# A four-layer transformer kernel on one core: modulation units in three parts, written order for a tail's second stream, an earlier context norm

## Chip, cores and metric

The kernel runs on one core of one Trainium2 chip. The metric is the device time of one execution in microseconds (us). PE is TensorE's matrix engine, DVE is VectorE, ACT is ScalarE, POOL is GpSimd, and SP is the engine whose queue issues the loads.

## The reference

Two latent streams of 256 tokens of 1024 features are worked on: the latents ("LAT") and a context ("CTX"). Four layers follow one another. The first two come from `first_block`, the others from `second_block` (one mLSTM layer, one sliding-window attention layer). Each layer computes its modulation from the condition vector, mixes tokens, and runs an MLP with a fourfold hidden width:

```python
mod = silu_c @ w_mod[l] + b_mod[l]                 # 1024 -> 6 * 1024, for latents and context
a = modulate(rms_norm(h, norm1_g[l]), sh1, sc1)    # h * (1 + scale) + shift
...
h = h + g1 * mix                                   # mix: pooling, gating unit, attention, or mLSTM
h = h + g2 * sq_relu_mlp(modulate(rms_norm(h, norm2_g[l]), sh2, sc2), w_ff1[l], w_ff2[l])
```

The context goes through the same steps in layers 1 and 3; layers 2 and 4 only read it.

## The kernel before

Everything is one program of `Builder` methods. Activations lie with features on partitions, in 8 tiles of 128 features by 512 columns: 256 of the context, 256 of the latents. Every operand of a large product is split into a high part and a low part (`whi` and `wlo` for weights), and three matmuls are issued for each 128x128 block: high by high, high by low, low by high. A weight block of 128x1024 is loaded by SP's queue into `raw`, copied by ScalarE to `whi`, and subtracted by VectorE (or the engine in `wlow`) to give `wlo`. `STAGES` gives each of `raw`, `mraw`, `whi` and `wlo` three buffers.

`gemm` takes the output tiles in turn; with `head=3` the first three run interleaved in `rows_of`, two steps apart (`SKEW`), so that TensorE has work while the inputs of the next step are made. With `tail` the last tiles run one stream after the other in `last_tiles`. `Steps` lets a norm's instructions (the mean rows, then the rstd rows of `ident`) be issued in between at given steps: `PRE` in heads, `MID` in tails. `issue_after` fixes the order of instructions; without it a scheduler picks, on each engine, the next instruction by its estimate of readiness.

The modulation is 352 units of 128 input features by 512 output features. One unit loads `mraw`, multiplies it by the condition and adds it to the sum `macc` on VectorE (context), multiplies it on ScalarE and adds it to a second sum on GpSimd (latents); after eight units a few small matmuls with `sel` reduce `macc` into `acc`. `drip` issues units between weight blocks at a rate `b.rate`, and `need(i, cg)` issues all that are left of a group when its result is wanted:

```python
    def one(self):
        self.pending.pop(0)[1]()

    def need(self, i, cg):
        while any(key == (i, cg) for key, _ in self.pending):
            self.one()
```

`block1` is layers 1 and 2 (l = 0 and 1), the mLSTM layer is layer 3, and the layer whose queries come from `project(t)` is layer 4.

## Time and profile before

| | |
|---|---|
| runs | 2252.66, 2251.72, 2252.01 us, median 2252.01 |
| profiled execution | 2251.2 us |
| its span, first to last instruction | 2249.3 us |
| mean granted TensorE clock | 0.986 |
| PE busy | 2179.0 us, 97% |
| DVE, ACT, POOL busy | 1617.5, 1155.4, 642.3 us |
| moved by DMA | 337.86 MB, mean 150 GB/s |

The profiled execution is one run with the profiler on; its span leaves out 1.9 us around the instructions. TensorE's busy share is an average: in the MLPs it is full, and between them it waits. A clock of 1.00 is 2.4 GHz, of 0.50 is 1.2 GHz.

### The profile page before, as it was taken

How to read it: one execution, taken by the hardware profiler on the slowest of the kernel's cores; microseconds unless marked ns; L12 is line 12 of the kernel's file. 1: busy time of each engine (PE TensorE's matmuls, PEld its weight loads, DVE VectorE, ACT ScalarE, POOL GpSimd, SP SyncE). 2: the span in 40 equal slices, each digit the busy share in tenths (PEclk: the TensorE clock that was granted, in tenths of full speed). 3: DMA queues.
4: the chain of work that ended last, by engine and by line, in shares of the span. 5: the costliest groups of instructions: out<-in, count | busy, mean ns of one | idle time of the engine just before them, and what ended most of it. 6: DMA issues, size and time to landing. Idle time of an engine off the chain costs nothing.

```text
span 2249.3 us, 36790 instructions
## 1 busy us (share of the span) xinstructions
PE 2179.0 (97%) x13602; PEld 1861.3 (83%) x13602; DVE 1617.5 (72%) x2830; ACT 1155.4 (51%) x2176; POOL 642.3 (29%) x529
## 2 busy tenths in 40 slices
PE   9899999999999989998999999999999999999998
PEld 7777877887777778898999977778777778879998
DVE  5876656777666986789777766678775566697776
ACT  4556434544443456655555665645444433676453
POOL 1630534524221542045000234262232122421000
PEclk9999999999999999999999999999999999999999
DMA  8451535445565443367554323444455552214552
GB/s 296 140 167 36 169 122 190 144 133 183 191 193 162 147 154 127 120 215 254 166 186 151 113 85 104 142 142 131 137 187 177 173 168 80 76 48 143 186 179 93
DMA packets 129011, 337.86 MB, mean 150 GB/s; under 512 B 15040, under 2 KB 24256, under 8 KB 128832
## 3 DMA queue, kind: packets, MB, share of 16 engines
q1 hardware_dynamic: 128832, 335.51, 46.0%
q8 instruction: 108, 1.77, 0.3%
q14 instruction: 71, 0.58, 0.1%
HBM read 334.40 MB, written 1.05 MB: 149 GB/s over the span
## 4 chain that ended last, share of the span: by engine, by line
PE 46%; DVE 4%; ACT 2%; issue 2%; POOL 1%; DMA 0%; DVEq 0%; POOLq 0%; ACTq 0%
PE mm L124 28%; PE mx L124 11%; PE S L124 2%; PE T L124 1%; PE num L124 1%; PE pv L124 1%; PE T L128 1%; DVE wlo L132 1%; ACT whi L118 1%; PE acc L124 0%; POOL macc L480 0%; DMA mraw<-wmod_in 0%; PE kv L124 0%; DVE B L121 0%; ACT W L118 0%
## 5 line engine op out<-in xcount | busy, mean ns | idle before, releaser
L124 PE MATMUL mm<-A,whi 128*128 128x512 f32 (+2 forms) x2632 | 666.2, 340 | 4.9 <-DVE A L121 1.5
L480 POOL TENSOR_TENSOR macc<-macc,mraw 128x512 f32<-128x512 f32 x244 | 361.9, 1483 | 757.3 <-ACT mraw L118 744.8
L124 PEld LDWEIGHTS mm<-A,whi 128*128 128x128 f32 x2632 | 449.3, 190 | 69.0 <-issue 10.0
L124 PE MATMUL mm<-B,whi 128*128 128x512 f32 (+2 forms) x1916 | 461.4, 331 | 2.8 <-DVE h L121 1.0
L132 DVE TENSOR_TENSOR wlo<-raw,whi 128x1024 fp32r<-128x1024 f32 x255 | 350.8, 1378 | 140.7 <-ACT whi L118 139.6
L124 PE MATMUL mm<-A,wlo 128*128 128x512 f32 (+2 forms) x1316 | 444.4, 338 | 1.2 <-DVE wlo L132 1.2
L118 ACT ACTIVATE whi<-raw 128x1024 fp32r<-128x1024 f32 x267 | 281.2, 1055 | 250.5 <-PE mm L124 154.6
L124 PEld LDWEIGHTS mm<-B,whi 128*128 128x128 f32 x1916 | 322.1, 189 | 41.8 <-issue 3.0
L118 ACT ACTIVATE mraw<-mraw,silu 128x512 f32<-128x512 f32 x244 | 175.5, 723 | 303.1 <-DVE macc L121 181.3
L124 PE MATMUL mx<-A,whi 128*128 128x512 f32 (+2 forms) x1272 | 323.3, 341 | 5.5 <-ACT whi L118 4.2
L124 PE MATMUL mm<-B,wlo 128*128 128x512 f32 (+2 forms) x958 | 315.2, 330 | 1.1 <-DVE wlo L132 1.1
L121 DVE SCALAR_TENSOR_TENSOR macc<-mraw,silu,macc 128x512 f32<-128x512 f32 x244 | 250.2, 1025 | 58.8 <-DMA mraw<-wmod_in 56.3
L124 PEld LDWEIGHTS mm<-A,wlo 128*128 128x128 f32 x1316 | 249.4, 190 | 29.2 <-DVE wlo L132 2.0
L132 DVE TENSOR_TENSOR wlo<-Y,whi 128x1024 fp32r<-128x1024 f32 x160 | 207.7, 1298 | 78.7 <-ACT whi L118 78.5
L118 ACT ACTIVATE whi<-Y 128x1024 fp32r<-128x1024 f32 x160 | 168.9, 1055 | 177.8 <-PE mm L124 124.7
L124 PEld LDWEIGHTS mx<-A,whi 128*128 128x128 f32 x1272 | 218.6, 190 | 35.1 <-ACT whi L118 4.4
L124 PE MATMUL mx<-A,wlo 128*128 128x512 f32 (+2 forms) x636 | 216.3, 340 | 0.7 <-DVE wlo L132 0.7
L124 PE MATMUL mx<-B,whi 128*128 128x256 f32 (+2 forms) x852 | 203.9, 327 | 3.0 <-DVE B L121 1.3
L124 PEld LDWEIGHTS mm<-B,wlo 128*128 128x128 f32 x958 | 181.1, 189 | 19.9 <-DVE wlo L132 2.0
L121 DVE SCALAR_TENSOR_TENSOR h<-mm,mod,h 128x256 f32<-128x256 f32 x278 | 125.5, 478 | 65.0 <-PE mm L124 64.6
L124 PEld LDWEIGHTS mx<-B,whi 128*128 128x128 f32 x852 | 144.3, 191 | 19.9 <-DVE B L121 2.7
L551 POOL TENSOR_TENSOR sums<-sums,T 128x256 f32<-128x256 f32 x60 | 65.6, 1100 | 307.5 <-ACT T L118 306.3
(331 smaller groups left out, 3009.8 us busy)
## 6 DMA issues: line engine op xcount, KB each, us to landing
mraw<-wmod_in SPq DMA_DIRECT2D x352, 256.0 KB, 2.9
Y<-ff_in SPq DMA_DIRECT2D x160, 512.0 KB, 3.6
raw<-ff_in SPq DMA_DIRECT2D x96, 512.0 KB, 3.5
raw<-win_in SPq DMA_DIRECT2D x68, 512.0 KB, 3.8
raw<-mwin_in SPq DMA_DIRECT2D x17, 512.0 KB, 3.5
raw<-wo_in SPq DMA_DIRECT2D x16, 512.0 KB, 4.3
raw<-swin_in SPq DMA_DIRECT2D x10, 512.0 KB, 3.5
B<-wfirst_in SPq DMA_DIRECT2D x16, 256.0 KB, 6.7
```

The lines of the kernel that those rows point to most:

```text
L118: return self.nc.scalar.activation(out, in_, func, **kw)
L121: return self.nc.vector.scalar_tensor_tensor(out, a, scalar, b, op0, op1)
L124: return self.nc.tensor.matmul(out, lhsT=lhsT, rhs=rhs, start=start, stop=stop, **kw)
L128: return self.nc.tensor.transpose(out, in_, self.ident[:k, :k])
L132: (eng or self.nc.vector).tensor_sub(lo, src, hi.bitcast(F32))
L480: self.nc.gpsimd.tensor_add(a1, a1, raw)
L551: (adder or self.nc.gpsimd).tensor_add(sums, sums, sq)
```

## The change

Five things are edited. A modulation unit becomes a generator in three parts: its load; the sum on VectorE; the product on ScalarE with the sum on GpSimd. `one` issues the last part of the unit before, then the load of this unit and of the next where they aren't out yet, then this unit's sum on VectorE. `rows_of` keeps the written order whenever it has steps, not only after a given instruction, and `last_tiles` hands the tail's second stream the last instruction before it until the steps are through. `MID` goes from (6, 12) to (8, 14). Layer 1 drips no units until its v rows. Layer 2's context norm is issued at `NEXT` = (2, 5) inside the first three tiles instead of behind them, and the loads of the next weights with it. Layer 4's first two query weights get their low parts on VectorE.

```diff
--- before.py
+++ after.py
@@ -38,7 +38,9 @@
 FIRST = (3, 3, 3, 3, 5, 7, 7, 7, 7), (2, 2, 2, 2, 4, 6, 6, 6, 6), (1, 1, 1, 1, 3)
 
 WARM = 40
-PRE, MID = (4, 7), (6, 12)
+PRE, MID = (4, 7), (8, 14)
+
+NEXT = (2, 5)
 PLAIN = (3, 6)
 
 SOONER = 70
@@ -57,6 +59,9 @@
             ins = next(self.parts, None)
         return ins
 
+    def done(self):
+        return self.n >= self.at[-1]
+
     def finish(self):
         for _ in self.parts:
             pass
@@ -67,6 +72,7 @@
         self.tc, self.nc, self.io = tc, tc.nc, io
         self.n = 0
         self.pending, self.owed, self.rate = [], 0.0, 0.0
+        self.begun, self.loaded = None, []
         self.raws = cycle(["raw"])
         self.ready, self.late = [], []
         self.banks = cycle(["mm", "mm", "mx"])
@@ -167,7 +173,7 @@
 
         last = len(xs) - 1
         order = after and (lambda ins=after: self.tc.issue_after(ins.ins))
-        strict = bool(after)
+        strict = bool(after or steps)
         for i in range(r0, r1 + SKEW * (len(tiles) - 1)):
             for j, (ps, (d, w)) in enumerate(zip(pss, tiles)):
                 i0 = i - SKEW * j
@@ -185,18 +191,18 @@
                     part = steps.tick()
                 ins = part or ins
                 order = lambda ins=ins: self.tc.issue_after(ins.ins)
-            elif steps:
-                steps.tick()
         return ins
 
-    def group(self, tiles, ks_of, xs, cols, evac, steps=None):
-
-
+    def group(self, tiles, ks_of, xs, cols, evac, steps=None, after=None):
+
+
+        ins = None
         for a, e in cols:
             pss = [self.ps(next(self.banks))[:, :e - a] for _ in tiles]
-            self.rows_of(pss, tiles, ks_of, xs, 0, len(xs), a, e, steps)
+            ins = self.rows_of(pss, tiles, ks_of, xs, 0, len(xs), a, e, steps, after)
             self.flush()
             self.take(pss, tiles, a, e, evac)
+        return ins
 
     def take(self, pss, tiles, a, e, evac):
 
@@ -207,7 +213,7 @@
                     self.late.append(part)
 
     def gemm(self, aps, xs, c0, evac, head=0, tail=0, order=(LAT, CTX), pre=None, mid=None, flush=True,
-             ahead=(), streams=True):
+             ahead=(), streams=True, at=PRE):
 
 
 
@@ -223,7 +229,7 @@
                      for j in range(m)]
             if i + m == n:
                 self.ready = [self.wload(ap, KT) for ap in ahead]
-            steps = Steps(pre, PRE) if pre and i == 0 else None
+            steps = Steps(pre, at) if pre and i == 0 else None
             self.group(tiles, ks_of, xs, cols[:1], evac, steps)
             if steps:
                 steps.finish()
@@ -245,9 +251,13 @@
 
     def last_tiles(self, tiles, ks_of, xs, by_stream, evac, mid):
         steps = Steps(mid, MID) if mid else None
+        last = None
         for s, cols in enumerate(by_stream):
             for tile in tiles:
-                self.group([tile], ks_of, xs, [cols], evac, steps if s else None)
+                due = s and steps and not steps.done()
+                ins = self.group([tile], ks_of, xs, [cols], evac, steps if due else None,
+                                 last if due else None)
+                last = ins
         if steps:
             steps.finish()
 
@@ -462,7 +472,9 @@
         w, sc = self.io[f"wmod{i}"], self.silu[i // 2]
 
         def unit(cg, half, k):
+
             raw = self.staged(w[cg, k][:, half * 512:half * 512 + 512], 512, cycle(["mraw"]))
+            yield
             a0, a1 = self.macc[:, 0], self.macc[:, 1]
 
             alone = i % 2 == 1 and cg >= 2
@@ -472,6 +484,7 @@
                     self.nc.vector.tensor_scalar_mul(a0, raw, sc[:, k, s:s + 1])
                 else:
                     self.stt(a0, raw, sc[:, k, s:s + 1], a0, ALU.mult, ALU.add)
+            yield
             if not alone or k % 2:
                 if k < 2 - (not alone):
                     self.act(a1, raw, scale=sc[:, k, LAT:LAT + 1])
@@ -495,8 +508,7 @@
         out = []
         for cg in groups:
             for half in range(2):
-                out += [((i, cg), (lambda cg=cg, half=half, k=k: unit(cg, half, k)))
-                        for k in range(KT)]
+                out += [((i, cg), unit(cg, half, k)) for k in range(KT)]
         return out
 
     def drip(self):
@@ -508,12 +520,27 @@
         self.owed = min(self.owed, 1.0)
 
     def one(self):
-        self.pending.pop(0)[1]()
+
+
+        self.rest()
+        self.begun = self.pending.pop(0)[1]
+        for piece in [self.begun] + [u for _, u in self.pending[:1]]:
+            if piece not in self.loaded:
+                next(piece)
+                self.loaded.append(piece)
+        self.loaded.remove(self.begun)
+        next(self.begun)
+
+    def rest(self):
+        if self.begun:
+            next(self.begun, None)
+        self.begun = None
 
     def need(self, i, cg):
 
         while any(key == (i, cg) for key, _ in self.pending):
             self.one()
+        self.rest()
         while self.late:
             self.flush()
 
@@ -886,7 +913,7 @@
         b.perm1 = b.load(ph, "perm1")
         b.icnt = b.load(ph, "icnt")
     pscale = b.vec[l][:, 64:66]
-    b.rate = 0.0 if l else RATES[l][0]
+    b.rate = 0.0
     win = io[f"win{l}"]
 
     qs, kh, kl = [], [], []
@@ -948,9 +975,7 @@
     if l == 0:
         pre(evac_first)
     else:
-        b.gemm(aps[:3], xs, c0, evac_first, head=3)
-        b.ready = [b.wload(ap, KT) for ap in aps[3:]]
-        b.whole(pre)
+        b.gemm(aps[:3], xs, c0, evac_first, head=3, pre=pre, at=NEXT, ahead=aps[3:])
         b.gemm(aps[3:4], xs, c0, lambda j, *r: evac_first(j + 3, *r))
     b.gemm_rows(aps[4:], L, xs, ("T", "T", "S", "S")[c0 // P:], evac_vs, c0=c0)
     br = b.new_xs("B", 4)
@@ -1393,9 +1418,10 @@
     def project(t):
         b.gemm([win[t]], xs, L, lambda _, ps, a, e: qs.append(query(ps)))
 
-    b.wlow = nc.gpsimd
     project(0)
     for t in range(8):
+        if t == 1:
+            b.wlow = nc.gpsimd
         if t < 7:
             project(t + 1)
         a = b.new_xs("A", 1)[0]
```

How this moves instructions is shown at three places. A name such as `T<-mm` is output from input; numbers are those of tiles and differ between the two programs.

First, VectorE at the tail of layer 3's output projection, before, up to the pair sum (L558) and the norm's small `sm`:

```order
L132 TENSOR_TENSOR wlo_15568<-raw_15565,whi_15567 128x1024
L121 SCALAR_TENSOR_TENSOR macc<-mraw_16180,silu_72,macc 128x512
L121 SCALAR_TENSOR_TENSOR h<-mx_15571,mod_97,h 128x256
L121 SCALAR_TENSOR_TENSOR macc<-mraw_16185,silu_72,macc 128x512
L121 SCALAR_TENSOR_TENSOR h<-mm_15600,mod_97,h 128x256
L121 SCALAR_TENSOR_TENSOR macc<-mraw_16229,silu_72,macc 128x512
L121 SCALAR_TENSOR_TENSOR h<-mm_15628,mod_97,h 128x256
L558 TENSOR_TENSOR T_3078_15626<-T_3078_15626,T_3080_15654 128x256
L568 TENSOR_SCALAR sm_15681<-T_15676 128x2
```

and of the change (the pair sum is L585 there):

```order
L127 SCALAR_TENSOR_TENSOR macc<-mraw_15527,silu_72,macc 128x512
L127 SCALAR_TENSOR_TENSOR h<-mm_15492,mod_97,h 128x256 x2
L138 TENSOR_TENSOR wlo_15545<-raw_15542,whi_15544 128x1024
L127 SCALAR_TENSOR_TENSOR h<-mx_15548,mod_97,h 128x256
L127 SCALAR_TENSOR_TENSOR h<-mm_15577,mod_97,h 128x256
L127 SCALAR_TENSOR_TENSOR h<-mm_15605,mod_97,h 128x256
L585 TENSOR_TENSOR T_3074_15603<-T_3074_15603,T_3076_15631 128x256
L127 SCALAR_TENSOR_TENSOR h<-mx_15634,mod_97,h 128x256
L595 TENSOR_SCALAR sm_15664<-T_15659 128x2
```

Three modulation sums (`macc<-mraw`) stood among the gate sums `h` ahead of the pair sum; now the last one stands before two `h`, a low part and three more `h`.

Second, TensorE at the start of layer 2, before, where the rstd rows of the norm (`T<-ident`) are issued:

```order
L124 MATMUL mm_7644<-A_7316,wlo_7583 128x256
L124 MATMUL mm_7644<-A_7318,whi_7582 128x256
L124 MATMUL mm_7644<-A_7319,whi_7582 128x256
L124 MATMUL mm_7644<-A_7318,wlo_7583 128x256
L124 MATMUL T_7607<-ident_118,sm_7604 128x128 x2
L124 MATMUL mm_7644<-A_7320,whi_7582 128x256
L124 MATMUL mm_7644<-A_7321,whi_7582 128x256
L124 MATMUL mm_7644<-A_7320,wlo_7583 128x256
L124 MATMUL mm_7644<-A_7322,whi_7582 128x256
```

and of the change:

```order
L130 MATMUL mm_7457<-A_7267,wlo_7424 128x256
L130 MATMUL mx_7458<-A_7263,whi_7429 128x256
L130 MATMUL mx_7458<-A_7264,whi_7429 128x256
L130 MATMUL T_7496<-ident_118,sm_7472 128x128 x2
L130 MATMUL mx_7458<-A_7263,wlo_7430 128x256
L130 MATMUL mm_7459<-A_7259,whi_7435 128x256
L130 MATMUL mm_7459<-A_7260,whi_7435 128x256
L130 MATMUL mm_7459<-A_7259,wlo_7436 128x256
L130 MATMUL mm_7457<-A_7269,whi_7423 128x256
```

The rstd rows stood in the middle of the fourth tile (`mm_7644`, alone); now they stand in the middle of the first three tiles (`mx_7458`, `mm_7459` and `mm_7457` in turn). The mean rows ahead of them move likewise.

Third, ScalarE at layer 1's queries, before (`T<-mx` is the copy of a query tile that the rotation needs, `Y` what becomes of it):

```order
L118 ACTIVATE T_271_1390<-acc_1381 128x128
L118 ACTIVATE Y_1357<-T_265_1359 64x256 x2
L118 ACTIVATE mraw_1559<-mraw_1559,silu_71 128x512
L118 ACTIVATE T_277_1424<-mx_1398 128x256
L118 ACTIVATE Y_1423<-mx_1398 64x256
L118 ACTIVATE whi_2212<-raw_2210 128x1024
L118 ACTIVATE Y_1423<-mx_1398 64x256
```

and of the change, up to the first products:

```order
L124 ACTIVATE T_252_1295<-mm_1269 128x256
L124 ACTIVATE Y_1294<-mm_1269 64x256 x2
L124 ACTIVATE Y_1294<-T_253_1296 64x256 x2
L124 ACTIVATE whi_2154<-raw_2152 128x1024
L124 ACTIVATE T_263_1350<-mx_1324 128x256
L124 ACTIVATE Y_1349<-mx_1324 64x256 x2
L124 ACTIVATE Y_1349<-T_264_1351 64x256 x2
L124 ACTIVATE whi_2191<-raw_2189 128x1024
L124 ACTIVATE T_275_1410<-mm_1384 128x256
L124 ACTIVATE Y_1409<-mm_1384 64x256
L124 ACTIVATE macc<-mraw_1375,silu_71 128x512
L124 ACTIVATE mraw_1441<-mraw_1441,silu_71 128x512
```

A modulation product (`mraw<-mraw`) stood right ahead of the copy `T<-mx`; now the first three `T` copies come with no product among them, and the products follow the third.

## Rows read from the trace of the kernel before

**Rows 1.** the page: span, and busy time of the engines

```profile
span 2249.3 us, 36790 instructions
...
PE 2179.0 (97%) x13602; PEld 1861.3 (83%) x13602; DVE 1617.5 (72%) x2830; ACT 1155.4 (51%) x2176; POOL 642.3 (29%) x529
```

**Rows 2.** windows (columns in the second line; PEclk is the granted clock)

```profile
core 0: us, PE busy (x) PEld busy (x) DVE busy (x) ACT busy (x) POOL busy (x), PEclk, DMA share, GB/s
82.00:89.00 7.00, 5.51 (x36) 4.40 (x37) 6.28 (x10) 6.30 (x13) 3.24 (x4) 0.51 0.52 140
...
829.00:840.00 11.00, 5.99 (x25) 5.27 (x26) 10.94 (x18) 3.63 (x7) 3.35 (x5) 0.53 0.45 153
1512.00:1519.00 7.00, 6.88 (x32) 6.88 (x33) 2.42 (x6) 1.36 (x2) 2.17 (x2) 0.52 0.25 64
...
550.00:700.00 150.00, 150.00 (x684) 119.15 (x683) 97.80 (x141) 61.83 (x87) 40.97 (x29) 1.00 0.59 190
```

**Rows 3.** waits of TensorE: total us, times, longest us

```profile
PE T L124 <- DVE T L558: 6.4, 3, 3.7
PE T L124 <- ACT E L118: 6.0, 2, 5.7
PE T L124 <- ACT T L118: 4.8, 5, 2.1
PE mx L124 <- ACT whi L118: 4.2, 1, 4.2
...
PE S L124 <- DVE wlo L132: 2.8, 1, 2.8
...
PE T L128 <- DVE E L1170: 2.2, 2, 1.1
PE mm L124 <- ACT T L118: 2.1, 1, 2.1
```

**Rows 4.** timeline, layer 1's keys: start, us, engine, line [idle <- releaser]

```profile
80.48 0.72 DVE L121 SCALAR_TENSOR_TENSOR macc<-mraw,silu,macc 128x512 f32<-128x512 f32 x1
...
81.29 0.72 ACT L118 ACTIVATE mraw<-mraw,silu 128x512 f32<-128x512 f32 x1 [4.28 <-DVE sm L942]
...
82.86 0.57 ACT L118 ACTIVATE E<-mm 128x512 f32<-128x512 f32 x1
```

**Rows 5.** timeline, layer 1's queries, ScalarE and TensorE

```profile
140.46 0.72 ACT L118 ACTIVATE mraw<-mraw,silu 128x512 f32<-128x512 f32 x1 [3.12 <-issue]
...
148.72 1.04 ACT L118 ACTIVATE whi<-raw 128x1024 fp32r<-128x1024 f32 x1
149.79 0.38 ACT L118 ACTIVATE T<-mm 128x256 f32<-128x256 f32 x1
```

**Rows 6.** timeline, start of layer 2

```profile
824.82 0.33 SPq L143 DMA_DIRECT2D raw<-win_in  x1
...
829.06 2.05 ACT L118 ACTIVATE whi<-raw 128x1024 fp32r<-128x1024 f32 x2
...
825.50 3.11 DVE L121 SCALAR_TENSOR_TENSOR T<-h,A,T 128x256 f32<-128x256 f32 x5 [0.71 <-ACT T L118]
833.97 1.21 DVE L132 TENSOR_TENSOR wlo<-raw,whi 128x1024 fp32r<-128x1024 f32 x1
```

**Rows 7.** timeline, head of layer 1's up projection, VectorE

```profile
437.70 1.21 DVE L132 TENSOR_TENSOR wlo<-Y,whi 128x1024 fp32r<-128x1024 f32 x1
```

**Rows 8.** timeline, tail of layer 3's output projection, VectorE

```profile
1508.82 0.75 DVE L121 SCALAR_TENSOR_TENSOR macc<-mraw,silu,macc 128x512 f32<-128x512 f32 x1 [3.19 <-DMA mraw<-wmod_in]
...
1510.79 1.28 DVE L558 TENSOR_TENSOR T<-T,T 128x256 f32<-128x256 f32 x1 [0.82 <-ACT T L118]
```

**Rows 9.** timeline, start of layer 4, three engines

```profile
1919.76 2.37 POOL L132 TENSOR_TENSOR wlo<-raw,whi 128x1024 fp32r<-128x1024 f32 x1 [4.22 <-ACT whi L118]
...
1920.32 2.10 DVE L771 TENSOR_TENSOR T<-T,T 128x256 f32<-128x256 f32 x1
```

**Rows 10.** instructions on macc: ns min/median/max, first and last start

```profile
L480 POOL TENSOR_TENSOR macc<-macc,mraw x244: 1262/1308/2863, 55.2 to 1859.4; 128x512 f32<-128x512 f32 x122
```

## The prediction

> **What bounds the kernel now.** I read the page's busy times first. TensorE is busy 2179.0 of 2249.3 us [rows 1], so 70.3 us of idle time, a slow clock and the matmuls themselves are all that there is to win. Then the windows: in the long MLP stretches TensorE is busy all the time at a granted clock of 1.00, and nothing is to be had there; between them lie short stretches at 0.51 to 0.53, which is the lower of the clock's two levels, 1.2 GHz beside 2.4 [rows 2]. Such a stretch costs what its busy time loses: from 82 to 89 us (1 − 0.51) × 5.51 = 2.7 us, from 829 to 840 us 0.47 × 5.99 = 2.8, from 1512 to 1519 us 0.48 × 6.88 = 3.3. Each lies at one of TensorE's long waits, so a wait costs itself and often some 3 us behind it. The list of waits [rows 3] names who ends them, and the timelines around the longest [rows 4 to 6, 8, 9] what the releaser itself stood behind. The reader is to see one pattern in them: a modulation product or sum (`mraw`, `macc`), which nobody needs soon, stands ahead of the instruction that TensorE waits for.
>
> **The change, part by part.** No matmul, copy or load is added beyond a handful of rows; the sum is of waits that go and waits that come.
>
> (a) Layer 1's keys. TensorE waits 5.7 us for the copy E [rows 3], which runs from 82.86 to 83.43; on ScalarE it stands behind a product that waited 4.28 us and started at 81.29, when the sum at 80.48 was done, and a weight copy [rows 4]. At stake are 5.7 + 2.7 = 8.4 us. In three parts the unit's load no longer goes out in the same turn as its sum, and in layer 1 no unit is dripped before the v rows; yet seven products still stand ahead of this E in the new order. I take 40%, **−3.5**; bounds 0 (the seven are as slow as now) and −8.4.
>
> (b) Layer 1's queries. Of five waits for a T copy (4.8 us in all, [rows 3]) two of some 2 us lie here. ScalarE reached the first copy behind a product at 140.46 that had idled 3.12 us; the second came at 149.79, right behind a product and a weight copy [rows 5]. The new order has the T copies ahead of the products (the third piece of order above). I take **−4.0**, nearly both; bounds 0 and −5.
>
> (c) Start of layer 2. TensorE waits 4.2 us for a high part and 2.8 us for a low part [rows 3]; the first ends when ScalarE's two copies from 829.06 end, at 831.11, the second when VectorE's low part from 833.97 ends, at 835.18 [rows 6]. That low part stands behind the context's modulation, which began at 825.50. With the norm's rows inside the head, the modulation starts some 6 us sooner (an estimate: its T rows stand about 50 matmuls sooner, and 684 took 150.00 us [rows 2], with half as many columns in many here), and the 2.8 us go. The 4.2 us mostly stay: the weights' load is issued at 824.82, a buffer's release sets that, and the copies could hardly run before 828. I take 2.8 + 1.2 = **−4.0**; bounds +1 (TensorE only arrives sooner at the late load, and the clock falls the same) and −(4.2 + 2.8 + 2.8) = −9.8.
>
> (d) Tail of layer 3's output projection. The longest wait for VectorE's pair sum is 3.7 us [rows 3]: a modulation sum waited 3.19 us for its load and started at 1508.82, and the pair sum could start only at 1510.79 and took 1.28 [rows 8]. In the new order no modulation sum stands within five instructions ahead of it (first piece of order), and MID moves the mean rows six matmuls later, 6 × 150.00 / 684 = 1.3 us at most. With the clock 3.7 + 3.3 = 7.0 us are at stake. Written order keeps TensorE from filling at the second tail tile, whose four mean rows now stand together; for that I keep back 2.5: **−4.5**, bounds −1 and −7.
>
> (e) Start of layer 4. TensorE waits 2.1 us for a T copy [rows 3]. GpSimd's low part (1919.76, 2.37 us) stands ahead of a rope product, and VectorE's rope sum took 2.10 us beside it, until 1922.42 [rows 9]. A low part on VectorE takes 1.21 [rows 7], so two of them there cost 2.4 us of an engine with room, and the 2.37 on GpSimd is gone. I take **−2.0**, bounds +1 (VectorE's two low parts hold the rope chain instead) and −4 (the clock behind it too).
> A rule speaks against this edit. The Trainium skill, SBUF — State Buffer, "SBUF: two separate sides", says that VectorE with two SBUF inputs and GpSimd take a shared port pair as an exclusive lock, the later one blocking until the other ends. The 2.10 us beside the low part of GpSimd look like that lock. By it VectorE's low parts would hold up GpSimd's rope products in turn, by 1.21 us each, and this term would be −2.0 + 1.2 = −0.8, the sum −15.3.
>
> (f) Layer 3's v rows (2.2 us in two waits for E, [rows 3]): the column copies stand a weight block sooner and behind no sum. Together with the end of layer 2: **−1.5**, bounds 0 and −3.
>
> (g) Written order at the heads. Until now TensorE filled with the other tiles when a low part was late. At layer 1's up head the pair sum and the modulation are followed by the second tile's low part at 437.70, 1.21 us long [rows 7]; in written order TensorE waits there. I price it at one low part, at two heads (layers 1 and 3): 2 × 1.21 = **+2.4**; bounds 0 and two low parts each with 1.7 us of clock (about half of a low stretch as above), 2 × (2.42 + 1.7) = +8.2.
>
> (h) Late units. With no drip at layer 1's start and three turns a unit, some ten units are done later and are caught up at layer 3's end by `need`. An add on GpSimd is 1.308 us [rows 10]; eight units are 10.5 us of GpSimd, mostly under 24-matmul blocks. I take **+0.6**; bounds −1 and +4. Where no stall lies, as in the MLPs, the units' new places cost nothing: TensorE is full there, VectorE is at 97.80 of 150 us and GpSimd at 40.97 [rows 2]. In a full burst that cover would be gone, at 1.3 us a unit.
>
> Sum: −3.5 − 4.0 − 4.0 − 4.5 − 2.0 − 1.5 + 2.4 + 0.6 = −16.5 us. The profiled execution took 2251.2 us, 1.9 more than its span; the median of the runs is 2252.0, 0.8 above it. So 2251.2 − 16.5 + 0.8 = **2235.5 us**.
>
> **The rivals.**
> *The queue only moves.* Seven products still stand ahead of layer 1's E, and each wait of the strict kind gives back part of what (a) and (b) win. Then only (c) and (d) remain, −8.5, with +2.4 of (g): 2252.0 − 6.1 = 2246. For it: no engine does less. Against it: order rows at the queries and at layer 3's tail show the products gone from there.
> *Parts bring nothing.* `mraw` has three buffers, and now three units can hold one (loaded, in its sums, waiting for its last part). The load on SP's queue then waits for the buffer, and weights behind it wait too, as now. (a), (b) and (f) become 0, and (c) and (d) are halved by the late weights: −4.3 − 2.0 + 2.4 + 0.6 = −3.3, 2249.
> *Slower: written order stalls.* Some dozen heads and tails issue strictly now. A stall of two low parts (2.4 us) and 1.7 of clock is 4.1 us. Gains of (a) to (f) are 19.5; at five stalls they are spent, and at six the kernel is slower by 5: with seven, 2252 − 19.5 + 28.7 = 2261. For it: in the heads TensorE does go around late rows now. Against it: most tails show no such wait near them.
>
> **How the numbers follow.** Forecast as summed: 0.56, with its own range 2227 to 2244, from the bounds of (a), (c) and (g) not all at one end. Queue only moves 0.22 (2241 to 2248). Parts bring nothing 0.13 (2247 to 2254). Written order stalls 0.09 (2253 and up). A measurement of this kernel can tell about 0.2%, 4.5 us, from no change. Faster by more: all of the first case, nearly all of the second, a little of the third, 0.78; within 0.2%: 0.13; slower: 0.09. The range 2225 to 2249 leaves out half of the third, the fourth and the lowest end.
>
> **What would show it.** TensorE's waits: the entries for T<-DVE T, T<-ACT E and T<-ACT T should fall from 6.4, 6.0 and 4.8 us to about 3, 3 and 1; the wait for a high part should stay at 2 to 4 us; windows 82:89 and 1512:1519 should have a clock above 0.7. New waits for a low part at the up heads of 1 to 3 us each would show (g). Wrong would be: idle time in all as now, near 70 us, or waits for acc behind GpSimd's adds in layer 3.

## The result, and the profile after

The changed kernel takes 2269.57 us (median of four runs, 2267.64 to 2271.46) beside 2251.86 for the kernel before on the same chip: 1.0082 times as long, 95% interval 1.0067 to 1.0097. It is slower by 18 us where 16.5 us of gain were forecast; the profiled execution took 2271.46 us with a span of 2269.7. The page's totals, which answer to [rows 1]:

```profile
span 2269.7 us, 36792 instructions
PE 2186.5 (96%) x13602; PEld 1869.9 (82%) x13602; DVE 1616.4 (71%) x2832; ACT 1156.8 (51%) x2176; POOL 625.1 (28%) x527
```

TensorE is idle for 2269.7 − 2186.5 = 83.2 us instead of 70.3, and busy 7.5 us longer, with as many matmuls: the mean clock fell from 0.986 to 0.981. The list of TensorE's waits answers to [rows 3] (us in all, times, longest):

```profile
PE T L130 <- ACT E L124: 10.3, 3, 6.5
PE mm L130 <- DVE wlo L138: 8.8, 6, 2.9
PE T L130 <- DVE T L585: 6.3, 3, 3.4
PE mx L130 <- DVE wlo L138: 5.5, 4, 2.7
PE S L130 <- ACT E L124: 4.7, 6, 2.9
...
PE T L130 <- POOL sums L578: 2.8, 2, 2.4
PE T L130 <- ACT T L124: 2.6, 4, 1.9
```

Of the three kinds of wait that were to fall only those for a T copy did, 4.8 to 2.6; those for the pair sum (T<-DVE T) stand at 6.3 where 6.4 was, and those for E, to be halved, grew. The low parts of VectorE, which were to bring 1 to 3 us at each of two heads, stand at 8.8 + 5.5 us in ten waits. The windows of [rows 2], one beside the second of them, and five more around new waits:

```profile
core 0: us, PE busy (x) PEld busy (x) DVE busy (x) ACT busy (x) POOL busy (x), PEclk, DMA share, GB/s
82.00:89.00 7.00, 4.95 (x38) 4.00 (x39) 6.59 (x7) 6.86 (x13) 5.81 (x5) 0.61 0.65 191
821.00:829.00 8.00, 6.66 (x34) 6.58 (x35) 5.35 (x9) 1.40 (x4) 1.60 (x2) 0.57 0.46 162
829.00:840.00 11.00, 7.97 (x66) 7.57 (x64) 9.68 (x16) 7.81 (x15) 1.38 (x1) 1.00 0.39 127
1512.00:1519.00 7.00, 7.00 (x39) 6.00 (x38) 5.92 (x7) 3.74 (x6) 6.92 (x5) 1.00 0.47 151
161.00:166.00 5.00, 3.15 (x10) 2.60 (x11) 3.90 (x12) 3.71 (x7) 1.28 (x1) 0.66 0.83 253
427.00:433.00 6.00, 4.27 (x20) 4.27 (x21) 3.90 (x5) 2.02 (x4) 3.87 (x5) 0.64 0.43 123
876.00:880.00 4.00, 3.40 (x8) 2.74 (x9) 3.62 (x6) 3.82 (x10) 1.28 (x1) 0.50 0.34 115
1541.00:1547.00 6.00, 4.54 (x21) 4.54 (x22) 4.44 (x8) 0.86 (x3) 0.88 (x1) 0.54 0.48 152
1922.00:1927.00 5.00, 4.11 (x22) 4.11 (x23) 3.65 (x7) 0.24 (x1) 0.88 (x1) 0.68 0.49 149
```

The low clock left 1512:1519, moved from 829:840 to the stretch ahead of it (0.57) and came up at four others; the same stretches of the kernel before, shifted by some us, have 1.00 and a full TensorE. The last window is no new place: there the kernel before has 0.50 already (1902 to 1907 us), with TensorE full. The MLP stayed as it was: from 560 to 710 us TensorE is busy for all 150.00 us at a clock of 1.00.

Some of this differs from one execution to the next. The run e5 below, which edits layer 4 alone, issues on every engine the same instructions in the same order as the kernel before until layer 4's rope products at some 1919 us. Yet a stretch of low clock in layer 3 that the one has, the other lacks (the kernel before, then e5):

```profile
1304.00:1311.00 7.00, 6.77 (x19) 5.39 (x20) 3.73 (x5) 2.55 (x4) 6.94 (x13) 0.51 0.36 116
1304.00:1311.00 7.00, 5.83 (x29) 4.50 (x30) 5.92 (x7) 3.27 (x6) 6.86 (x10) 1.00 0.38 130
```

To see where time went, the two traces were laid side by side. The table is worked out from them: at the moment when TensorE had started the same share of its matmul columns (reductions of the modulation left out), how many us a kernel is behind the kernel before. A step between two rows is what that stretch lost or won.

```
us before  after written  parts+late  norm,MID  parts  late  written  catch-up  late,fast       low parts, twice
                 (e7)     (e8)        (e9)      (e12)  (e13) (e14)    (e15)     (e18)           (e5)    (e19)
   130     -1.2   0.6     -0.4        -0.2      -0.9    1.9  -1.1      2.0       1.8             0.0     -0.8
   160     -5.1  -1.0     -2.9        -0.3      -1.5    1.2  -5.0     -0.8       2.0             0.0     -2.4
   180     -0.7  -1.0     -1.1        -0.3      -0.8    1.7  -0.6      1.2       4.3             0.0     -2.4
   400     -1.7  -1.0     -2.0        -0.2      -0.1    0.9  -1.4      0.3      37.5             0.1     -2.4
   460      6.4   0.9      3.7         0.5       3.9    5.0   5.7      7.0      46.5             0.3     -2.3
   780      6.1   1.1      3.2         0.6       5.3    4.7   5.5     32.8      47.9             1.7     -2.8
   860      6.1   0.3      4.5         3.3       4.4    5.9   6.0     41.0      47.3             1.0     -2.2
   900     12.7   0.3      4.4         5.0       4.5    6.0   8.8     40.9      47.3             1.0     -2.2
  1030     12.6   0.3      4.8         4.9       8.6    9.2   8.3     42.4      48.6             0.8     -2.1
  1100     18.1   3.1     10.2         7.5      10.9   16.0  13.4     42.7      47.8             2.0      2.1
  1290     18.3   2.7     10.0         7.5      10.7   16.0  13.8     42.6      47.6             2.0      1.8
  1325     14.1   1.2      5.8         4.5      16.9   11.9   9.4     39.6      53.4            -0.9      0.3
  1360     17.3   1.2      7.8         4.5      17.5   15.4  11.3     39.9      54.1            -0.9      0.3
  1500     19.7   0.9     10.5         4.3      17.0   19.0  13.0     39.6      53.6            -0.8      0.0
  1522     14.6  -0.2      5.4         2.8      17.0   13.8   8.0     37.4      47.4            -2.7     -0.9
  1545     19.4   3.3      5.4         3.3      17.0   13.9   9.5     37.4      51.3            -2.7     -0.9
  1880     19.7   3.3      5.7         3.6      16.7   14.8   9.9     34.2      46.8            -2.7     -1.0
  1908     22.6   6.1      6.5         0.5      17.3   15.2   8.7     33.7      44.2            -5.3     -3.6
  1950     20.1   5.1      6.7        -1.0      17.4   15.3   6.7     33.8      45.6            -6.9     -5.2
  2240     19.9   6.2      8.4         0.2      17.5   15.3   6.3     33.5      46.6            -7.0     -5.6
```

Each column rests on one execution. Runs of the kernel before lay between 2243.6 and 2255.4 us on the chips used. The last two columns tell what one execution is worth: e5 and e19 both have the order of the kernel before until 1919 us, and until 1880 us they still drift between −2.9 and +3.5 us, with steps of −2.9 (e5, 1290 to 1325) and +4.2 (e19, 1030 to 1100), and both win 2.6 between 1880 and 1908, ahead of their edit. So a single step of up to 4 us says little by itself; it counts where several kernels show it. In the changed kernel the stretches forecast to win do so at 130 to 160 (−3.9), 1290 to 1325 (−4.2), 1500 to 1522 (−5.1) and 1908 to 1950 (−2.5). Next to each a stretch loses: 160 to 180 (+4.4), 400 to 460 (+8.1), 860 to 900 (+6.6), 1030 to 1100 (+5.5), 1325 to 1360 (+3.2), 1522 to 1545 (+4.8), 1880 to 1908 (+2.9). How far other kernels bear these out is said at the terms of the prediction.

What stands ahead of the largest losses. In layer 1's last tail TensorE waits for VectorE's pair sum (VectorE's timeline, then TensorE's; idle time before a row and its releaser in brackets):

```profile
425.18 0.75 DVE L127 SCALAR_TENSOR_TENSOR macc<-mraw,silu,macc 128x512 f32<-128x512 f32 x1 [1.15 <-DMA mraw<-wmod_in]
427.14 1.53 DVE L585 TENSOR_TENSOR T<-T,T 128x256 f32<-128x256 f32 x1 [0.82 <-POOL macc L493]
```

```profile
428.73 0.59 PE L130 MATMUL T<-mean,T 128*128 128x1 f32 x2 [3.39 <-DVE T L585]
...
443.51 0.38 PE L130 MATMUL mx<-A,wlo 128*128 128x256 f32 x1 [2.73 <-DVE wlo L138]
```

It is the pattern of [rows 8], a modulation sum that waited for its load ahead of a pair sum, come up again at another tail; the last row is the low part of the up head. The pair sum itself took 1.53 us, where the median of the twelve on its line is 0.42, while GpSimd worked at three modulation sums:

```profile
423.99 4.41 POOL L493 TENSOR_TENSOR macc<-macc,mraw 128x512 f32<-128x512 f32 x3 [1.50 <-ACT mraw L124]
```

So some 1.1 of the 3.39 us (1.53 − 0.42) go with the units' part on GpSimd, running beside the pair sum (the last section has more such rows); the 1.28 us of [rows 8] are of the same kind, with GpSimd's sum of 1.27 us from 1510.52.

Layer 2's keys show a chain through three engines (VectorE, ScalarE, GpSimd, then TensorE):

```profile
871.07 0.75 DVE L127 SCALAR_TENSOR_TENSOR macc<-mraw,silu,macc 128x512 f32<-128x512 f32 x1
```

```profile
871.86 0.72 ACT L124 ACTIVATE mraw<-mraw,silu 128x512 f32<-128x512 f32 x1 [0.93 <-DVE macc L127]
874.71 0.42 ACT L124 ACTIVATE B<-B 128x256 fp32r<-128x256 f32 x1 [2.13 <-POOL B L994]
875.03 1.04 ACT L124 ACTIVATE whi<-raw 128x1024 fp32r<-128x1024 f32 x1
875.98 0.58 ACT L124 ACTIVATE E<-mm 128x512 f32<-128x512 f32 x1
```

```profile
872.72 1.27 POOL L493 TENSOR_TENSOR macc<-macc,mraw 128x512 f32<-128x512 f32 x1 [2.73 <-ACT mraw L124]
873.95 0.73 POOL L994 TENSOR_TENSOR B<-B,B 128x256 f32<-128x256 f32 x1
```

```profile
876.61 1.22 PE L130 MATMUL T<-E,perm 128*128 128x256 f32 x2 [3.52 <-ACT E L124]
```

One unit's three pieces now stand on VectorE, ScalarE and GpSimd in turn, and the last one, 1.27 us, stands ahead of a sum for which ScalarE's copy B waits, with a weight copy and E behind it.

### The profile page after: what moved, and what is told of

It reads as the page before. It is cut to its first block, busy times and chain, and to the rows that moved or that the text cites. A ratio compares the mean times of both kernels' runs of the same rounds, so it can differ in the third digit from the quotient of the medians.

```text
span 2269.7 us, 36792 instructions
## 1 busy us (share of the span) xinstructions
PE 2186.5 (96%) x13602; PEld 1869.9 (82%) x13602; DVE 1616.4 (71%) x2832; ACT 1156.8 (51%) x2176; POOL 625.1 (28%) x527
## 5 line engine op out<-in xcount | busy, mean ns | idle before, releaser
L493 POOL TENSOR_TENSOR macc<-macc,mraw 128x512 f32<-128x512 f32 x244 | 356.7, 1462 | 659.6 <-ACT mraw L124 646.6
```

What stands on the lines that cost most here:

```text
L493: self.nc.gpsimd.tensor_add(a1, a1, raw)
```

## The experiments

Three theories. *Order*: the written order costs some 20 us and the rest does what was forecast. *Units*: the modulation's new places cost it, in parts, late or both. *Backlog*, a finer form: fewer units are done early, they meet a critical place later, and done sooner they would cost nothing. In the texts put on record, theory A is Order, B, D, E and F are forms of Units, C is an early form of Backlog, and the Form theory is its opposite: the places themselves cost it, however many units are late. The four "up heads" near 443, 1080, 1542 and 1923 us are those of layers 1, 2 and 3 and, the last, the head of layer 4's keys. Each run is compared with the kernel before on its own chip; "after" and "before" say which kernel is edited.

**e1**, after without the written order:

```diff
-        strict = bool(after or steps)
+        strict = bool(after)
...
+            elif steps:
+                steps.tick()
...
-                ins = self.group([tile], ks_of, xs, [cols], evac, steps if due else None, last if due else None)
+                self.group([tile], ks_of, xs, [cols], evac, steps if s else None)
```

> The changed kernel without the written order: rows with steps follow the scheduler again, and the tail's second stream is not held behind the first; MID, the unit in parts, the later drip, the earlier norm and layer 4's low parts stay. Theory A (written order): TensorE waits for low parts at the four up heads (2.7 us near 443 us, 2.0 near 1080, 2.9 near 1542, 2.3 near 1923) and for the pair sum near 429 us (3.4), each with a stretch of half clock; without it these go and the time is 2250 to 2256 us. Theory B (the unit in parts has put sums ahead of what TensorE needs): the waits near 163 us, 877 us and 1040 to 1052 us stay, and the time is still 2262 or more.

Measured: 2259.45 us, 1.0048 [1.0035, 1.0061]. Some 8 of the 18 us go (0.34% of 2250); the rest stays. Order is part of it, not all.

**e2**, after with a unit issued whole:

```diff
-        self.rest()
-        self.begun = self.pending.pop(0)[1]
...
-        next(self.begun)
+        for _ in self.pending.pop(0)[1]:
+            pass
```

> The changed kernel with each modulation unit issued whole, in one turn, as before. Theory A: the waits for low parts at the up heads stay, the time is 2262 to 2270 us. Theory B: the waits near 163 us (2.9 us), 877 us (3.5 us) and 1040 to 1052 us (3.3 us in four) go, each with its half clock, and the time is 2253 to 2258 us.

Measured: 2273.59 us, 1.0116 [1.0101, 1.0131]. Given the rest of the change, the parts help a little.

**e4**, after with layer 1 dripping from its start:

```diff
-    b.rate = 0.0
+    b.rate = 0.0 if l else RATES[l][0]
```

> The changed kernel with layer 1 dripping from its start (rate 1.4), as before. Theory C (units kept back pile up): fewer sums are left for layer 1's attention and for the tail of its output projection, so that the waits near 163 us (2.9 us) and near 429 us (3.4 us) go, with their half clock, and the time is 2258 to 2263 us. Theories A and B: it stays at 2266 to 2271 us.

Measured: 2276.0 us, 1.0128 [1.011, 1.0145]. Undoing the late drip makes it worse too.

**e7**, before with the written order alone, in heads and tails:

```diff
-        strict = bool(after)
+        strict = bool(after or steps)
...
-            elif steps:
-                steps.tick()
...
-                self.group([tile], ks_of, xs, [cols], evac, steps if s else None)
+                ins = self.group([tile], ks_of, xs, [cols], evac, steps if due else None, last if due else None)
```

> The kernel before with the written order alone (rows with steps, and the tail's second stream), MID at (6, 12). Theory A: the waits for low parts at the up heads come, and the time is 2262 to 2268 us. Theory B: little happens, 2250 to 2256 us.

Measured: 2256.99 us, 1.0044 [1.0027, 1.0062]. It fits e1, and the list of TensorE's waits names the price (e7, then the kernel before):

```profile
PE mm L130 <- DVE wlo L138: 8.5, 6, 3.8
PE mx L130 <- DVE wlo L138: 5.6, 5, 2.8
```

```profile
PE mx L124 <- DVE wlo L132: 2.6, 4, 1.2
PE mm L124 <- DVE wlo L132: 2.3, 4, 0.7
```

**e3**, after with layer 2's norm behind the first three tiles, and **e9**, before with the earlier norm, the new MID and layer 4's low parts:

```diff
-        b.gemm(aps[:3], xs, c0, evac_first, head=3, pre=pre, at=NEXT, ahead=aps[3:])
+        b.gemm(aps[:3], xs, c0, evac_first, head=3)
+        b.ready = [b.wload(ap, KT) for ap in aps[3:]]
+        b.whole(pre)
```

> The changed kernel with layer 2's context norm behind the first three tiles, as before. If the earlier norm costs what the ledger of the change shows at layer 2 (the wait of 2.4 us for GpSimd's sums near 822 us, and the new wait of 3.5 us for a key copy near 877 us with its half clock), the time falls by 4 to 8 us against the changed kernel, to 1.0045 to 1.0065 of the kernel before. If the earlier norm gives what the prediction said (4 us), it rises by 2 to 4 us.

> The kernel before with the earlier norm of layer 2, MID at (8, 14) and layer 4's low parts on VectorE, no written order and whole units. Theory A or D: 2 to 8 us faster than before, from layer 4's start (2 us wait gone) and layer 3's output tail. If the norm is the cost: slower by 0 to 5 us, with the loss between 810 and 880 us.

Measured: e3 2266.58 us, 1.0075 [1.0052, 1.0098], as after; e9 2249.14 us, 1.0000 [0.9986, 1.0014]. The three small edits bring nothing that can be told, and for the earlier norm neither a gain nor a loss is shown.

**e10**, before with MID and layer 4's low parts, and **e5**, before with those low parts alone:

```diff
-PRE, MID = (4, 7), (6, 12)
+PRE, MID = (4, 7), (8, 14)
```

```diff
-    b.wlow = nc.gpsimd
     project(0)
     for t in range(8):
+        if t == 1:
+            b.wlow = nc.gpsimd
```

> As the run before, without the earlier norm: MID at (8, 14) and layer 4's low parts alone. 3 to 7 us faster than before: 2 to 4 us at the start of layer 4, and 1 to 3 us at layer 3's output tail, where mean rows come six matmuls later.

> The kernel before with layer 4's first two low parts on VectorE alone: the wait of 2.1 us near 1924 us goes and half the stretch of low clock behind it, 2 to 4 us faster. By the shared port's rule it would be 0 to 2 us faster, since VectorE's low parts hold GpSimd's rope products.

Measured: e10 2249.19 us, 0.9999 [0.9988, 1.0011]; e5 2247.44 us, 0.9995 [0.998, 1.0009]. MID is worth nothing that can be told. Between 1908 and 1950 us the low parts win 1.4 to 1.6 us in either trace ((e) below); the medians can't tell that.

**e8**, before with units in parts and the late drip; **e12**, the parts alone; **e13**, the late drip alone. The parts are the change's own edit of the unit and of `one`, the late drip is one line:

```diff
 def one(self):
-    self.pending.pop(0)[1]()
+    self.rest()
+    self.begun = self.pending.pop(0)[1]
...
-    b.rate = 0.0 if l else RATES[l][0]
+    b.rate = 0.0
```

> The kernel before with the unit in three parts and layer 1's later drip alone. Theory A (written order is most of the loss): faster than before by 2 to 6 us. Theory D (units kept back stand before the tails and heads that come next: waits near 429 us, 163 us, 877 us): slower by 4 to 10 us, with these waits in its trace.

> The kernel before with the unit in three parts alone; layer 1 drips from its start as before. Theory E (the parts are the cost: a unit's last part comes one turn late and its group ends later): slower by 6 to 11 us, with units behind the kernel before from 330 us on. Theory F (the later drip is the cost: eight units fewer at any time): within 3 us of before, and the count of sums done follows the kernel before.

> The kernel before with layer 1's drip starting at the v rows alone, units whole. Theory F: slower by 6 to 11 us, eight units behind from 120 us on, with the wait near 428 us (pair sum behind modulation sums) and those near 1040 and 1072 us. Theory E: within 3 us of before.

Measured: e8 2257.93 us, 1.0048 [1.0031, 1.0066]; e12 2268.35 us, 1.0072 [1.0047, 1.0098]; e13 2265.96 us, 1.0072 [1.0053, 1.009]. Each alone costs 16 us and both together 11; the intervals overlap, so that the two together cost less than either isn't shown. With e7 the pieces of the change add up: 0.44 + 0.48 + 0 = 0.92% beside 0.82% measured. So Units is the other half. The table says that they lose in different places: the parts between 1290 and 1325, where the changed kernel wins; the late drip at 1030 to 1100 (e13 +6.8, though e19 has +4.2 there in the old order) and between 1325 and 1500. The parts' loss from 1290 to 1325 (e12 +6.0) is one wait with the low clock behind it (0.51 from 1328 to 1342 us), and its chain is the old pattern: a unit's load, its sum on VectorE, its product on ScalarE, and behind that the copy that TensorE waits for:

```profile
1322.91 0.75 DVE L127 SCALAR_TENSOR_TENSOR macc<-mraw,silu,macc 128x512 f32<-128x512 f32 x1 [7.33 <-DMA mraw<-wmod_in]
1323.75 0.72 ACT L124 ACTIVATE mraw<-mraw,silu 128x512 f32<-128x512 f32 x1 [4.87 <-DVE macc L127]
1329.35 0.92 PE L130 MATMUL kv<-Q,T 128*64 128x129 f32 x6 [5.86 <-ACT Q L124]
```

e4, the other kernel with parts and the early drip, has this wait too, at 5.9 us, and so has e18, with whole units done sooner, at 5.8; in e8, with parts and the late drip, it is 1.0.

**e14**, after with the written order in the tails only:

```diff
-        strict = bool(after or steps)
+        strict = bool(after)
...
+            elif steps:
+                steps.tick()
```

> The changed kernel with the written order in the tails' second stream alone; in heads the scheduler picks again. If the heads hold the cost of the written order, the waits for low parts at the up heads (near 443, 1080, 1542 and 1923 us) go or fall below 1 us, and the time is as without any written order, 1.0040 to 1.0055 of the kernel before. If the tails hold it, it stays at 1.0075 to 1.0090.

Measured: 2258.78 us, 1.0033 [1.002, 1.0046], no more than e1, and for a plain reason: the traces of e14 and e1 have the same instructions in the same order on every engine, so `last_tiles` as edited moves nothing here, and the two are one order measured twice. The written order that costs is that of the heads. Layer 1's up head isn't where: e14 loses as much up to 460 us (table), with a wait of 2.3 us for VectorE's modulation (mm<-DVE A) in place of the one for the low part. It costs at layer 2's keys, at the up head of layer 3 and at the head of layer 4's keys, where e14 loses less than after by 3.8, 3.3 and 4.1 us, and e1 by 4.9, 4.3 and 2.7.

**e15**, e8 with a faster drip in layer 1's MLP, **e17**, e14 with the same, **e16**, e5 with a faster drip in layer 1's mixing, and **e18**, e13 with a much faster one there:

```diff
-RATES = ((1.4, 2.0),
+RATES = ((1.4, 2.6),
```

(e16: 2.0, 2.0; e18: 2.6, 2.0.)

> The kernel before with the unit in three parts and the later drip, and 2.6 units a block instead of 2.0 in layer 1's MLP, where TensorE is full and the other engines have room. Backlog theory: the eight units are caught up by 800 us, and of the loss of 8.4 us the part behind 800 us (four waits near 1040, those near 1072, 1338 and 1485) goes, 2249 to 2253 us on this scale; the wait near 428 us stays. Form theory: the waits behind 800 us stay, 1.004 to 1.006.

> The changed kernel with written order in tails alone, and 2.6 units a block in layer 1's MLP. Backlog theory: the losses behind 1000 us near the gates and norms go, 0.997 to 1.001. Form theory: 1.002 to 1.005 as without the faster rate.

> The kernel before with layer 4's first two low parts on VectorE, and 2.0 units instead of 1.4 a block in layer 1 ahead of the MLP. If units done sooner gain, 0.995 to 0.999; if they collide with layer 1's copies and gates, 1.001 to 1.005, with new waits between 80 and 430 us.

> The kernel before with layer 1's later drip, units whole, and 2.6 units a block from the v rows on to the MLP. Backlog theory: by 400 us the count of sums is that of the kernel before, the wait near 428 us and all later ones are as before, and the time is within 4 us of before, what is left being between 100 and 400 us. Form theory: slower by 8 to 16 us, as with the slow rate.

Measured: e15 2282.81 us, 1.0151 [1.0133, 1.0168]; e17 2285.36, 1.0163 [1.0138, 1.0188]; e16 2274.74, 1.0125 [1.0102, 1.0147]; e18 2304.44, 1.0251 [1.0223, 1.0279]. Backlog falls in the form it was given. Its one half holds: once caught up, e15 loses next to nothing behind 860 us (its column goes from 41.0 to 33.5, in part because more reductions are already done by then, where e8's rises from 4.5 to 8.4). But units done sooner cost more than they save, since TensorE takes its reductions in the order in which they are issued and waits for sums that aren't there. Such waits on VectorE's and GpSimd's sums are 0.7 us in all in the kernel before; in e15, then in e18, they are:

```profile
PE acc L130 <- POOL macc L492: 12.3, 7, 2.2
PE acc L130 <- DVE macc L127: 3.5, 3, 1.7
```

```profile
PE acc L130 <- DVE macc L127: 12.7, 5, 4.4
PE acc L130 <- POOL macc L492: 7.4, 5, 1.9
```

**e20**, after with the second head tile's low part on GpSimd where a norm is issued inside the head:

```diff
-            tiles = [(i + j, self.ready.pop(0) if self.ready else self.wload(aps[i + j], kt))
+            tiles = [(i + j, self.ready.pop(0) if self.ready else
+                      self.wload(aps[i + j], kt, self.nc.gpsimd if pre and j == 1 else None))
```

> The changed kernel, with the low part of a head's second tile made by GpSimd instead of VectorE in five heads (three up heads among them, not layer 2's). If the late low part is what the written order pays for, the waits of 2.7, 2.9 and 2.3 us near 443, 1542 and 1923 us go or shrink below 1 us, and with their half clock the time falls by 8 to 12 us, to 1.003 to 1.005 of before. If not, other waits take their place and it stays above 1.007.

Measured: 2269.79 us, 1.0104 [1.0087, 1.0121], no better than after. The waits of 2.73, 2.91 and 2.29 us are gone and others stand in their place. By the comparison of the table e20 loses 3.0 us less than after at layer 4's keys, and 6.5 more at the first product of layer 3, where GpSimd's own low part now comes late and the clock behind it is 0.53 (1271 to 1282 us; 1.00 in the changed kernel):

```profile
1269.50 0.39 PE L130 MATMUL mm<-A,wlo 128*128 128x256 f32 x1 [1.32 <-POOL wlo L138]
```

GpSimd's timeline and then VectorE's, at layer 1's up head:

```profile
437.39 2.38 POOL L138 TENSOR_TENSOR wlo<-Y,whi 128x1024 fp32r<-128x1024 f32 x1 [3.22 <-ACT whi L124]
```

```profile
437.75 2.30 DVE L127 SCALAR_TENSOR_TENSOR A<-T,mod,A 128x256 fp32r<-128x256 f32 x1
439.98 0.47 DVE L127 SCALAR_TENSOR_TENSOR T<-h,A,T 128x256 f32<-128x256 f32 x1
```

**e19**, before with the written order in the tails and layer 4's low parts on VectorE, which were taken for the parts that cost nothing:

```diff
+                ins = self.group([tile], ks_of, xs, [cols], evac, steps if due else None, last if due else None)
...
+        if t == 1:
+            b.wlow = nc.gpsimd
```

> The kernel before with the written order in tails and layer 4's first two low parts on VectorE. If both keep what they showed alone, 2 to 5 us faster, 0.9978 to 0.9991; if placement noise eats it, within 0.1% of before.

Measured: 2245.85 us, 0.9992 [0.9983, 1.0001], over five rounds. The traces of e19 and e5 have the same order on every engine, so the tails add nothing and e19 is e5 measured again, 0.9992 beside 0.9995. It is the best version found; the interval just reaches 1, so it isn't shown to beat the kernel before.

## Why the prediction was wrong

The forecast fails at two terms that were mis-sized, (g) and (h), and at one idea behind (a), (b), (c) and (d): that a wait taken away stays away. The slower rival, given 0.09, had the right sign, and its cause, written order in the heads, is about half of the loss; the other half, the units' new places, it didn't have. The rival that the queue only moves named the give-back, but let it eat only the gains of (a) and (b). Up to 440 us the changed kernel, e1, e3, e14, e17 and e20 have one order on every engine; these are the six executions of (a) and (b).

(a) Layer 1's keys, −3.5: failed; the bound of 0 was near (−1.2 by 130 us; the six executions lie between −1.2 and +1.4). The wait for E grew from [rows 3]'s 5.7 to 6.5. ScalarE's rows show the same order as [rows 4]:

```profile
81.84 0.72 ACT L124 ACTIVATE mraw<-mraw,silu 128x512 f32<-128x512 f32 x1 [3.30 <-DVE macc L127]
82.47 1.04 ACT L124 ACTIVATE whi<-raw 128x1024 fp32r<-128x1024 f32 x1
83.42 0.58 ACT L124 ACTIVATE E<-mm 128x512 f32<-128x512 f32 x1
```

The 40% should have been read from the order: the last product ahead of E still waits for its sum.

(b) Layer 1's queries, −4.0: right in its place, −3.9 between 130 and 160, and given back at once. The six executions win 2.6 to 3.9 there and give back 2.0 to 4.5 by 180 us. TensorE now waits for the softmax. On VectorE a modulation sum stands inside its chain (DVE, then ACT, then PE):

```profile
160.44 0.75 DVE L127 SCALAR_TENSOR_TENSOR macc<-mraw,silu,macc 128x512 f32<-128x512 f32 x1
...
161.61 0.49 DVE L842 CUSTOM_DVE_ANT_0 S<-S,T,sm 128x256 f32<-128x256 f32 x1
```

```profile
162.01 0.69 ACT L124 ACTIVATE E<-S,sm 128x512 f32<-128x512 f32 x1
```

```profile
162.84 1.22 PE L130 MATMUL S<-Q,Y 128*128 128x512 f32 x2 [2.92 <-ACT E L124]
```

ScalarE's E starts as VectorE's step from 161.61 ends. The sum accounts for 0.75 of the 2.92 us; that the remainder is TensorE coming sooner to a chain that doesn't is argued, not shown. The clock is 0.66 behind it.

(c) Layer 2's start, −4.0: zero. Between 825 and 845 us the changed kernel wins 5.1 and between 780 and 825 it loses 5.1; e3, with the old norm, loses 1.7 and 1.4 there (the same comparison, at these two bounds). The mean rows inside the head meet their sums on GpSimd too soon (the 2.4 us for POOL sums in the list). The clock in 829:840 is 1.00, but the low clock only moved: it is 0.57 in 821:829, behind that wait. At the keys behind it the kernels that write this head lose, by the same comparison, 6.6, 5.7 (e2), 5.7 (e4) and 2.4 us (e20), those that don't 2.8 or less (e14, e1, e3); no term saw that.

(d) Layer 3's output tail, −4.5: right in its place, −5.1, and the clock in 1512:1519 is 1.00. MID isn't needed for it: e8, without MID, has −5.1 too, and of its halves e12 has 0 and e13, the late drip, −5.2. (e10, with MID and no change of units, has −4.5; the two don't add. e5, in the order of the kernel before, has −1.9, so not all of it is the change's.) The 2.5 us kept back for the written order of the tail had no reason: that edit moved no instruction (e14 and e1). The gain is given back by +2.4 before (the units' burst) and +4.8 at the up head:

```profile
1542.46 0.58 PE L130 MATMUL mm<-B,wlo 128*128 128x256 f32 x1 [2.91 <-DVE wlo L138]
```

(e) Layer 4's start, −2.0: right, as far as steps of this size can tell. The wait of 2.1 us for the T copy is 0.3 in the changed kernel and in e5, and still 2.1 in e7, which lacks the edit. Between 1908 and 1950 us the changed kernel wins 2.5, e5, e9, e10 and e19 1.4 to 1.7; e7, e8, e12 and e13, without the edit, lie between −1.0 and +0.2. What e5 and e19 win just ahead of it, 2.6, isn't the edit's: they still have the old order there. GpSimd's rope products now have no low part ahead, and VectorE's rows read:

```profile
1940.33 1.23 DVE L138 TENSOR_TENSOR wlo<-raw,whi 128x1024 fp32r<-128x1024 f32 x1 [1.96 <-ACT whi L124]
...
1941.80 1.22 DVE L138 TENSOR_TENSOR wlo<-raw,whi 128x1024 fp32r<-128x1024 f32 x1
1942.93 0.42 DVE L798 TENSOR_TENSOR T<-T,T 128x256 f32<-128x256 f32 x1
```

The rope sum takes 0.42 us where [rows 9] had 2.10. The counter price of 1.21 us didn't come, and the rule behind it wasn't put to the test at this place: GpSimd's rope products (1935.53, 2.56 us for two) were done before VectorE's low parts began at 1940.33, so the two never met.

(f) The v rows and the end of layer 2, −1.5: at the v rows the two waits for E are gone, but of the −4.2 there 2.9 are what e5 wins too, with both waits still there and no edit ahead of it, from the low clock that it lacks; 3.2 are lost at once at 1325 to 1360, and the end of layer 2 loses 5.5 (1030 to 1100) instead of winning, of which e19, in the old order, has 4.2.

(g) Written order at the heads, +2.4: the first failed step. e7 measures 0.44 [0.27, 0.62]%, 6 to 14 us; e1 against the changed kernel gives 8. The mechanism was named rightly, a low part late while TensorE may not fill, but it was priced at 1.21 us and two heads. It stands at 2.3 to 3.8 us a wait, with a slow clock behind it (0.54 in the window at 1541), and at the head of layer 4's keys too, which wasn't counted: e7 loses 3.5 us at 1522 to 1545 and 2.8 at 1880 to 1908. In the changed kernel the written head of layer 2 seems to add its part at the keys ((c)). The upper bound, +8.2, was near.

(h) Late units, +0.6: the second. Parts and late drip together cost 0.48 [0.31, 0.66]%, 7 to 15 us, above the bound of +4. The price was of units added to a burst; what counts is where all the others come to stand. e12 shows that it isn't a matter of how many are late: VectorE has done as many sums as before at 430 and at 1000 us (72 and 168), by 1325 us it has 190 beside 192, and the kernel still loses 16 us.

What stays open is why one place is hit and not the next: any shift of the units tried here, sooner, later, in parts or whole, ended slower, with its losses at places that differ from kernel to kernel. That the kernel before stands at a good point of this is what the runs show; a rule by which such a place could be told ahead they don't.

## What to carry to other kernels

When work that nobody needs soon is moved from one wait, look up which wait it will stand ahead of next, in the new order and on every engine that it touches; count a gain only if no such place comes up. Price a written order by the longest time that the late operand was ever late, with the clock behind it, times every head that it governs. And when a trace is to tell a small win in its place, find first what two executions of one and the same order differ by there (up to 4 us in a stretch here), and compare the order of instructions before calling two runs two experiments: an edit to the program may move none.

## What had not been expected of the hardware

VectorE is held up by GpSimd by nearly the whole length of an operation: in e20 a step that applies the modulation took 2.30 us, where the next one takes 0.47; it began 0.36 us after GpSimd's low part of 2.38 and ended 0.28 after it. The Trainium skill, SBUF — State Buffer, "SBUF: two separate sides", tells of such a lock on a shared port pair, the later one blocking; these rows agree with it, as does the rope sum of (e) with 2.10 against 0.42 us. The pair sums of 1.53 and 1.28 us against 0.42 are further such rows. The reverse stands in the trace of the kernel before: a GpSimd sum that started at 115.80 took 2.31 us, where [rows 10] has a median of 1.308, beside VectorE's low part of 1.21 us from 115.74. At layer 4's start the two didn't meet.
